# A hybrid decoder block on one core: the left sums of the first MLP product made by accumulating transfers, token loads in lots, m5 over two phases

## The chip, the core and the metric

One Trainium2 chip; the kernel runs on one core of it, as one program. The metric is the device time of one execution in microseconds (us). The core has the matmul engine (PE, with its weight loads PEld), VectorE (DVE), ScalarE (ACT), GpSimd (POOL), and SyncE (SP), which here only issues transfers. A wait in an engine's queue holds everything that stands behind it in that queue.

## What is computed

One decoder layer on x of 2048 tokens by 1024 channels, in float32: two mixers (dilated attention, chunked gMLP), merged by gates and an output product, then a squared-ReLU MLP. Each part has a norm before and behind. The part that the change touches is the MLP:

```
h = _rmsnorm(x, norm_pre_mlp)                         # 2048 x 1024
a = relu(einsum('bsd,df->bsf', h, w_mlp_in))          # 1024 -> 4096
y = einsum('bsf,fd->bsd', a * a, w_mlp_out)           # 4096 -> 1024
x = x + _rmsnorm(y, norm_post_mlp)
```

## The kernel before

**Stages.** Projections and attention; from about 1000 us the gates and the output product, called here the merge (`merge`, `out_block`), over four chunks of 512 tokens in the order 2, 3, 0, 1; from 1406 to 2028 us the first MLP product, the h stage; then the second, the y stage, to the end at 2660.6 us. A float32 product is made of three fp32r matmuls: each operand is split into a high part (a rounded copy, by ACT) and a low part (the difference, by DVE or POOL), and hi*hi, hi*lo and lo*hi are added in PSUM.

**Two levels of Strassen-Winograd.** The h stage replaces eight block products by seven at an outer level, and each of these again by seven. The seven outer products are the *phases*, in the order of `OUTER`: left operands A11, A12, S2, S1, S4, S3, A22, with Winograd numbers m = 1, 2, 6, 5, 3, 7, 4. A11 to A22 are quarters of `w_mlp_in`; S1 to S4 are sums of them. Right operands are quarters of the tokens or sums of them (T). Each phase has eight *steps* (q = 0 to 7, `HQ`), 56 in all (n); a step has seven *products* of six matmuls each (`hproduct`, line 1547). Steps overlap: the list `yorder` gives each product its place, so a step ends six places into the next. A place k is the unit of time of the schedule, and `later(k, f)` puts an instruction at a place.

**Order.** From the end of the merge the order is written out by hand (`as_written`): each engine runs its instructions in program order.

**The left operand of a step.** Before the stage, `w_piece` (13 times in the merge) and `w_load`, `w_sum`, `w_store` (3 times in phase 0) load a pair of weight blocks, make S2, S4, S3 and S1 with four adds, and store them in DRAM (`ws_d`). `load_ha` (line 1380) then brings one left operand of 512 KB into `hraw` (two buffers) with one SP transfer, from `w_mlp_in` or from `ws_d`. `sum_ha` calls `combine`: POOL makes the inner sums (lines 1389, 1390, 1395, 1396, 128x256 each), ACT the high parts (1391, 1397, 1400, 1404), DVE the low parts (1393, 1399, 1402, 1406). It writes `hs`, a ring of three. At the end of step n (place k) the sum of step n+3 is set to places k+1 to k+7 (`SUM_AT`), and the load of step n+5 to k+8. The y stage uses the same `combine` and the same places.

**The right operands of a phase.** `load_hb` (line 1446) brings 2 MB for the next phase in four transfers, all at place 7 of a phase (step 1). Where the operand is a difference (`LESS`, three phases), `less_load` (1450) fetches what is subtracted, 256 KB at a time, and `less_sub` (1454) subtracts it on DVE and POOL, the first 4 or 5 places after. `sum_w2` (POOL, 1474 to 1479) and `ops_hb` (ACT 1467, then DVE or POOL; line 1952 is the `f(*args)` that runs all that `later` holds) make the seven split operands. Most of these are made in the last step of the phase before.

**What becomes of a product.** It is added from PSUM to an accumulator X in SBUF, or in phases m = 2, 5, 3 to a tile `e` (lines 1559, 1561, 1563, mostly DVE). Products of one step share PSUM banks, so a product waits until the last one in its bank, four places before, is read. In phase m = 5 (phase 3, counted from 0), `e` is added to X (DVE and POOL, half each) and stored in `m5_d`; in phases 5 and 6 it is loaded again (`m5_load`, 1579) and subtracted from X (`m5_sub`, POOL, 1584), four tiles a step for eight steps. T sums of tokens come from `t_piece` in the merge and from `outer_load`, `outer_sum`, `outer_store`.

Of the kernel before, what the change touches and what calls it, by code (L numbers as in the profile page):

```python
# [17 lines left out]
P = 128  # L18
# [24 lines left out]
def block_kernel(ctx, tc, a, out):  # L43
# [106 lines left out]
    ws_d = dtile([NF // 4, P, 4, 2, 512], "wsd")  # L150
# [1135 lines left out]
    T_AT, WS_AT = ("T1", "T3", "T4", "T2"), ("S2", "S4", "S3", "S1")  # L1286
# [16 lines left out]
    def w_piece(t):  # L1303

        w, v = (ttp.tile([P, 2, 512], F32, name=f"{n}w{t}", tag=n, bufs=1) for n in ("tq", "tr"))
        for z, n in ((v, t + NF // 2), (w, t)):
            sp.dma_start(z.rearrange("p a c -> p (a c)"), a["w_mlp_in"][n].rearrange("p k c -> p (k c)"))
        yield
        a11, a12, a21, a22 = w[:, 0], w[:, 1], v[:, 0], v[:, 1]
        q, f = divmod(t, 2)  # L1310
        dve.tensor_add(a22, a21, a22)
        dve.tensor_sub(a21, a11, a21)
        pool.dma_start(ws_d[q][:, 2:4, f], v)
        dve.tensor_sub(a11, a22, a11)
        dve.tensor_sub(a12, a12, a11)
        pool.dma_start(ws_d[q][:, 0:2, f], w)
        yield

    W_EARLY = 13
    pieces = deque([w_piece(t) for t in range(W_EARLY - 2)] + [t_piece(0), t_piece(1)] +  # L1320
                   [w_piece(t) for t in range(W_EARLY - 2, W_EARLY)])
# [10 lines left out]

    c_now = [2]

    def merge_pieces(dt):
        if dt in ((0, 2, 4, 6, 7) if c_now[0] == 1 else (1, 3, 5, 7)):
            next_piece()
# [33 lines left out]
    def load_ha(n):  # L1371
        o, q = hsteps[n]
        name = OUTER[o][1]
        raw = hraw_[n] = r4.tile([P, 4, 256], F32, name=f"hraw_{n}", tag="sraw", bufs=2)
# [5 lines left out]
        sp.dma_start(raw.rearrange("p (f k) c -> p f (k c)", f=2), src)  # L1380

    def combine(n, w, raw):
# [11 lines left out]
        yield  # L1394
        pool.tensor_sub(a11, s5, a11)
        pool.tensor_sub(a12, a12, a11)
        act.activation(hi[:, 3], s5, AF.Copy)
        yield
        dve.tensor_sub(lo[:, 3], s5, f32(hi[:, 3]))
        act.activation(hi[:, 4], a21, AF.Copy)  # L1400
        yield
        dve.tensor_sub(lo[:, 4], a21, f32(hi[:, 4]))
        yield
# [36 lines left out]
    def load_hb(o):  # L1440

        name = ("B11", "B21", "T2", "B12", "B22", "B22", "B21")[o]
        for kk in range(2):
            raw = w2r_[o, kk] = l3.tile([P, 5, 512], F32, name=f"hb_{o}{kk}", tag="w2r", bufs=2)
            for kh in range(2):
                sp.dma_start(raw[:, 2 * kh:2 * kh + 2].rearrange("p c t -> p (c t)"), b_rows(name, kk + 2 * kh))
# [16 lines left out]
    def ops_hb(k, o, j, engs):  # L1463
        for m, eng in enumerate(engs):
            hi, lo = w2_[key(o, m), OPS[j]] = spot()
# [46 lines left out]
    def w_load(t):  # L1512

        outer_t["w", t] = [rx.tile([P, 512], F32, name=f"wt{t}{m}", tag="xs" if (t - W_EARLY) % 2 else "c1", bufs=4) for m in range(4)]
        for m, z in enumerate(outer_t["w", t]):
            sp.dma_start(z, a["w_mlp_in"][t + (0, 0, 16, 16)[m]][:, 4 * (m % 2):4 * (m % 2) + 4].rearrange("p k c -> p (k c)"))

    def w_sum(t, which):
        a11, a12, a21, a22 = outer_t["w", t]
        if which == 0:  # L1520
            dve.tensor_add(a22, a21, a22)
        elif which == 1:
            pool.tensor_sub(a21, a11, a21)
        elif which == 2:
            dve.tensor_sub(a11, a22, a11)
        else:
            pool.tensor_sub(a12, a12, a11)

    def w_store(t):
        q, f = divmod(t, 2)  # L1530
        s2, s4, s3, s1 = outer_t.pop(("w", t))
        for m, z in enumerate((s2, s4, s3, s1)):
            sp.dma_start(ws_d[q][:, m, f], z)

    def hproduct(k, n, i):
# [16 lines left out]
        if m in (2, 3, 5):  # L1552
            if first:
                stage_[n, f, c] = rx.tile([P, 512], F32, name=f"e{n}{f}{c}", tag="c1" if (f, c) == (0, 1) else "xs", bufs=4)
            t = stage_[n, f, c]
        else:
            t = x_
        if m in (1, 5) and first:
            act.activation(t, p, AF.Copy)
        elif m in (2, 3) and first:  # L1560
            dve.tensor_add(t, x_, p)
        else:
# [3 lines left out]
        if m == 5:  # L1566
            later(k + 1, (pool if c else dve).tensor_add, x_, x_, t)
# [4 lines left out]
              t.rearrange("p (i c) -> p i c", i=4))  # L1572

# [12 lines left out]
    def hstep(k, n, i):  # L1586
# [3 lines left out]
        if i == 1:  # L1590
            if q == 1:
                if o == 6:
                    for w in range(2):
                        load_w2(w)
                else:
                    load_hb(o + 1)
                    if o + 1 in LESS:
                        for b in range(4):
                            later(k + 6 * b + 1, less_load, o + 1, b)
                            for kk in range(2):  # L1600
                                later(k + 6 * b + 5 + kk, less_sub, o + 1, b, kk)
# [10 lines left out]
        if q == HQ - 1 and USE[i][0] < 6:  # L1612
            j = USE[i][0] + 1
            ops_hb(k, o + 1, j, (dve, dve if o in (0, 3) else pool))
# [4 lines left out]
    def spatial_out(dt):  # L1619
# [12 lines left out]
        merge_pieces(dt)  # L1632
# [16 lines left out]
    for n, c in enumerate(chunks):  # L1649
        if n:  # L1650
            c_now[0] = c
            mg = merge(c, yt, {0: flush, 2: flush}, merge_pieces)
        for i in range(4):
# [3 lines left out]
            if n < 3 or not i:  # L1657
                next_piece()
# [5 lines left out]
            if n == 3 and i == 1:  # L1664
# [25 lines left out]
                for n_ in range(2):  # L1690
                    outer_load(n_)
# [221 lines left out]
    for k in range(7):  # L1913
        at(k, s2)
    for k, f, args in ((0, first_split, (3, 0)), (1, flush, ()), (1, first_split, (3, 1)), (3, first_split, (4, 0)),
                       (4, first_split, (4, 1)), (6, first_split, (5, 0)), (7, first_split, (5, 1)), (7, load_ha, (4,)),
                       (8, first_split, (6, 0)), (9, first_split, (6, 1)), (9, flush, ())):
        later(k, f, *args)
    for n in range(8 + NF // 2 - W_EARLY):
        t = 5 * n - 5  # L1920
        load, one, store, z = (outer_load, outer_sum, outer_store, n) if n < 8 else (w_load, w_sum, w_store, W_EARLY + n - 8)
        if n > 1:
            later(t, load, z)
        for d, m in ((4, 0), (5, 1), (6, 2), (7, 3)):
            later(max(t + d, 0), one, z, m)
        later(t + 9, store, z)
    gfin = None
    for k, (_, stage, n, i) in enumerate(yorder):
# [40 lines left out]
        elif i in (3, ("p", 7)):  # L1969
            m = n + 3 + (NH if stage else 0)  # L1970
            if m < NH + len(ysteps):
# [6 lines left out]
                if m + 2 < NH + len(ysteps):  # L1978
                    later(k + 8, load_raw, m + 2)
# [75 lines left out]
```

## Time and profile before

| what | value |
|---|---|
| runs | 2664.3 us median of 3 (2658.52 to 2667.07) |
| profiled execution | 2662.48 us, its span 2660.6 us, clock granted 0.984 |
| busy | PE 97%, PEld 80%, DVE 69%, POOL 53%, ACT 41% of the span |
| DMA | 568.69 MB, 214 GB/s |
| merge after its first chunk, h stage, y stage | about 1106 to 1406, 1406 to 2028, 2028 to 2640 us |

The trace is of one execution. A row of a view by groups gives the line, engine, operation and tiles, the count behind x, busy us and mean ns of one, and the engine's idle time just before, with what ended it. A row of the timeline gives start and length, and in brackets the idle time before with its releaser. A row of windows gives, for a stretch, each engine's busy us and its instructions, the mean clock granted to PE, the busy share of the DMA engines, and GB/s.

### The profile page before, as it was taken

What the parts mean: (1) busy time and instruction counts of PE and PEld (TensorE: products, weight loads), DVE (VectorE), ACT (ScalarE), POOL (GpSimd) and SP (SyncE); (2) the same over time, 40 slices, a digit from 0 to 9 for tenths busy, and PEclk for the clock granted to TensorE, in tenths of its full rate; (3) what the DMA queues carried; (4) which work ended last, traced back from release to release, by engine and by line L of the source; (5) the groups of instructions that cost most, each with busy time, mean ns of one, the idle gap of its engine ahead of it and who ended that gap; (6) DMA issues with size and microseconds to landing.
All of it is one profiled execution on the core that took longest, in us unless ns stands there. A gap on an engine that the chain in (4) does not pass through costs nothing. (4 is left out here: it accounts for less than half of the span.)

```text
span 2660.6 us, 35654 instructions
## 1 busy us (share of the span) xinstructions
PE 2569.2 (97%) x12122; PEld 2139.0 (80%) x12122; DVE 1835.8 (69%) x3170; ACT 1095.7 (41%) x2318; POOL 1404.9 (53%) x1282
## 2 busy tenths in 40 slices
PE   9999999999999999899999999989889999999998
PEld 8888888888888887788877787867767888888886
DVE  5676665534433465866677888988768888788867
ACT  5213111254455444534435333433224555555555
POOL 0363354374464654111125566857877777777634
PEclk9999999999999999999999999999989999999999
DMA  8779768988888998867677652566764221222236
GB/s 321 283 247 322 266 227 291 301 280 253 291 281 238 242 301 317 317 234 260 232 266 268 197 170 93 178 186 188 235 210 150 88 87 56 88 87 87 88 114 211
DMA packets 412136, 568.69 MB, mean 214 GB/s; under 512 B 58801, under 2 KB 247473, under 8 KB 410930
## 3 DMA queue, kind: packets, MB, share of 16 engines
q1 hardware_dynamic: 385872, 502.63, 58.1%
q0 software_dynamic: 16192, 57.16, 5.5%
q10 hardware_dynamic: 9890, 6.62, 0.8%
q8 instruction: 96, 1.57, 0.2%
q14 instruction: 86, 0.70, 0.1%
HBM read 362.16 MB, written 204.14 MB: 213 GB/s over the span
## 5 line engine op out<-in xcount | busy, mean ns | idle before, releaser
L1547 PE MATMUL ha<-spot,hs 128*128 128x512 f32 x1344 | 345.2, 407 | 43.9 <-DVE X_yt L1563 17.6
L1547 PEld LDWEIGHTS ha<-spot,hs 128*128 128x128 f32 x1344 | 264.2, 198 | 106.4 <-issue 23.7
L1860 PE MATMUL ya<-spot,s 128*128 128x512 f32 x1344 | 325.7, 391 | 3.8 <-DVE X_yt L1868 3.8
L1860 PEld LDWEIGHTS ya<-spot,s 128*128 128x128 f32 x1344 | 253.8, 189 | 57.0 <-ACT sraw L1724 4.2
L1547 PE MATMUL hc<-spot,hs 128*128 128x512 f32 x672 | 175.0, 396 | 8.3 <-DVE X_xr L1563 3.4
L728 PE MATMUL g<-opA,spots 128*128 128x512 f32 x672 | 171.5, 399 | 1.8 <-DVE cv L760 1.8
L1860 PE MATMUL yc<-spot,s 128*128 128x512 f32 x672 | 170.6, 389 | 0.0
L1724 ACT ACTIVATE sraw<-sraw 128x1024 f32<-128x1024 f32 x128 | 134.4, 1050 | 83.5 <-DMA sraw<-sd 78.1
L728 PE MATMUL g<-opB,spots 128*128 128x512 f32 x648 | 164.0, 397 | 0.0
L1547 PEld LDWEIGHTS hc<-spot,hs 128*128 128x128 f32 x672 | 129.0, 193 | 37.9 <-DVE X_xr L1563 3.9
L96 PE MATMUL x<-hT_a,wq 128*128 128x512 f32 x384 | 149.7, 390 | 0.0
L97 PE MATMUL x<-hT_a,wq 128*128 128x512 f32 x384 | 149.4, 389 | 0.0
L98 PE MATMUL x<-hT_a,wq 128*128 128x512 f32 x384 | 149.4, 389 | 0.0
L1860 PEld LDWEIGHTS yc<-spot,s 128*128 128x128 f32 x672 | 126.4, 188 | 26.3
L728 PEld LDWEIGHTS g<-opA,spots 128*128 128x128 f32 x672 | 121.6, 189 | 24.1 <-issue 2.2
L79 POOL TENSOR_TENSOR spots<-gr,spots 128x512 fp32r<-128x512 f32 x98 | 127.8, 1308 | 22.1 <-PE g L728 7.9
L79 POOL TENSOR_TENSOR spot<-w2r,spot 128x512 fp32r<-128x512 f32 x79 | 120.9, 1553 | 34.7 <-ACT spot L71 34.7
L728 PEld LDWEIGHTS g<-opB,spots 128*128 128x128 f32 x648 | 116.9, 188 | 21.2
L71 ACT ACTIVATE hl<-r 128x512 fp32r<-128x512 f32 x48 | 30.4, 633 | 237.0 <-POOL r L329 89.0
L978 DVE TENSOR_REDUCE o<-po 128x256 f32<-128x512 f32 x48 | 33.2, 691 | 133.9 <-PE po L977 133.9
L73 POOL TENSOR_SCALAR spots<-gr 128x512 fp32r<-128x512 f32 x86 | 55.4, 644 | 132.0 <-PE g L728 93.4
L73 POOL TENSOR_SCALAR wq<-wq_r 128x1024 fp32r<-128x1024 f32 x24 | 31.9, 1335 | 138.2 <-PE va L98 87.6
(463 smaller groups left out, 6863.6 us busy)
## 6 DMA issues: line engine op xcount, KB each, us to landing
sraw<-sd SPq DMA_DIRECT2D x128, 256.0 KB, 3.3
qk<-hl SPq DMA_DIRECT2D x24, 1024.0 KB, 5.6
qq<-qk SPq DMA_DIRECT2D x96, 256.0 KB, 5.1
sd<-e SPq DMA_DIRECT2D x64, 256.0 KB, 4.7
hraw<-wsd SPq DMA_DIRECT2D x32, 512.0 KB, 4.5
w2r<-in_w_mlp_out_dram SPq DMA_DIRECT2D x16, 1024.0 KB, 6.5
g<-gated SPq DMA_DIRECT2D x56, 256.0 KB, 5.6
gr<-sgd SPq DMA_DIRECT2D x53, 256.0 KB, 4.8
```

Source lines behind the costliest of these rows:

```text
L71: act.activation(hi, src, AF.Copy)
L73: pool.tensor_scalar(hi, src, 1.0, 1.0, op0=OP.mult, op1=OP.mult)
L79: (pool if lo_eng == "pool" else dve).tensor_sub(lo, src, f32(hi))
L96: pe.matmul(ps, lh, rh, start=start, stop=False)
L97: pe.matmul(ps, lh, rl, start=False, stop=False)
L98: pe.matmul(ps, ll, rh, start=False, stop=stop)
L728: pe.matmul(p, w[:, l, k], h[:, r, k], start=i in (1, 6, 5, 4) and not k and not m, stop=k == 3 and m == 2, skip_group_check=True)
L978: dve.tensor_reduce(ot[:, :, j * 64:(j + 1) * 64], po.rearrange("p (b h e) -> p b e h", b=4, h=2), axis=AX.X, op=OP.add)
L1547: pe.matmul(p, w[:, l, S_AT[i], kk * P:(kk + 1) * P], b[r], start=i in (1, 2, 5) and not kk and not z, stop=kk == 1 and z == 2, skip_group ...
L1724: act.activation(sraw_[n], sraw_[n], func)
L1860: pe.matmul(p, s[:, l], w[r], start=i in (1, 2, 5) and not m and not o, stop=m == 1 and o == 2, skip_group_check=True)
```

## The change

1. `w_piece`, `w_load`, `w_sum`, `w_store` and `ws_d` go. In the merge only the two `t_piece` stay, in the four blocks of the third chunk. The eight `outer_load` groups start at place 4 and come every 5 places (before: two ahead of the stage, the rest from place 5).
2. `load_ha` takes terms. The first comes over SP; the others are added onto the tile by transfers that POOL issues with `accum_op=OP.add`. S2 = A21 + A22 - A11, S1 = A21 + A22, S4 = A12 - S2, S3 = A21 - A11. S3 has the other sign than before, so the products of m = 7 are subtracted. The load moves from k+8 to k+6; the added terms are at k+9 and k+12.
3. The negatives of A11 and S2 are made by `negate` on ACT at the start of `sum_ha` in phase A11 and phase S2 (one 128x1024 into an X tile that is not in use yet, or two 128x512), and stored over SP (512 KB a step, 16 steps).
4. `combine` takes five places instead of seven.
5. `load_hb` is cut into four: places 4, 8, 11 and 15 of a phase. `less_load` starts at place 16 and comes every 5 places instead of 6; each `less_sub` is 4 places behind its load.
6. Of the second split operand, one half is made in step 6 instead of step 7, on POOL instead of DVE in most phases.
7. In phase m = 5 the half that POOL added to X is added by an accumulating transfer inside SBUF (`collect`), issued by POOL. `e` tiles are spread evenly over two tags.
8. `m5_load` and `m5_sub` come every 9.5 places instead of 7: from step 44 to the end of step 54.

```diff
-    ws_d = dtile([NF // 4, P, 4, 2, 512], "wsd")
+    neg_d = {name: dtile([NF // 4, P, 2, 512], f"neg{name}d") for name in ("A11", "S2")}
...
-    pieces = deque([w_piece(t) for t in range(W_EARLY - 2)] + [t_piece(0), t_piece(1)] +
-                   [w_piece(t) for t in range(W_EARLY - 2, W_EARLY)])
+    pieces = deque([t_piece(0), t_piece(1)])
...
+    TERMS = dict(S2=("A21", "A22", "-A11"), S1=("A21", "A22"), S4=("A12", "-S2"), S3=("A21", "-A11"))
+
+    def load_ha(n, term=0):
         o, q = hsteps[n]
+        terms = TERMS.get(OUTER[o][1], (OUTER[o][1],))
+        if term >= len(terms):
+            return
+        name = terms[term]
...
-            src = ws_d[q][:, WS_AT.index(name)]
-        sp.dma_start(raw.rearrange("p (f k) c -> p (f k) c", f=2), src)
+            src = neg_d[name[1:]][q]
+        if term:
+            pool.dma_start(raw, src, accum_op=OP.add)
+        else:
+            sp.dma_start(raw, src)
+
+    def negate(n):
+
+        o, q = hsteps[n]
+        name, raw = OUTER[o][1], hraw_[n]
+        dst = neg_d[name][q].rearrange("p f c -> p (f c)")
+        if name == "A11" and q > 1:
+            z = [X[(0, 0, 8, 9, 12, 13, 14, 15)[q]]]
+        else:
+            z = [rx.tile([P, 512], F32, name=f"neg{n}{m}", tag="xs", bufs=4) for m in range(2)]
+        w = D // len(z)
+        for m, t in enumerate(z):
+            act.activation(t, raw.rearrange("p k c -> p (k c)")[:, m * w:(m + 1) * w], AF.Copy, scale=-1.0)
+        return [(dst[:, m * w:(m + 1) * w], t) for m, t in enumerate(z)]
...
-        yield from combine(n, w, hraw_.pop(n))
-
-    SUM_AT = (1, 2, 3, 4, 5, 6, 7)
+        kept = negate(n) if OUTER[hsteps[n][0]][1] in neg_d else []
+        yield from staged(combine(n, w, hraw_.pop(n)), kept)
...
+    SUM_AT = (1, 2, 3, 4, 5)
...
-            later(k + 1, (pool if c else dve).tensor_add, x_, x_, t)
+            if c:
+                later(k + 1, collect, x_, t)
+            else:
+                later(k + 1, dve.tensor_add, x_, x_, t)
...
+    def collect(to, t):
+        pool.dma_start(to, t, accum_op=OP.add)
...
-            q5 = n - 5 * HQ - 3
-            if 0 <= q5 < HQ:
-                for f in range(2):
-                    later(k + 3 * f, m5_load, q5, f)
-                    later(k + 4 + 2 * f, m5_sub, q5, f)
...
+        if i == 6 and not q and o < 6:
+            for m in range(4):
+                later(k + (0, 4, 7, 11)[m], load_hb, o + 1, *divmod(m, 2))
+            if o + 1 in LESS:
+                for m, b in enumerate((0, 1, 3, 2)):
+                    later(k + 12 + 5 * m, less_load, o + 1, b)
+                    for kk in range(2):
+                        later(k + 16 + 5 * m, less_sub, o + 1, b, kk)
+        if i == 6 and q == 6:
+            ops_hb(k, o + 1, 1, (dve if o in (0, 3) else pool, None))
...
+    for q in range(HQ):
+        t = 7 * (5 * HQ + 4) + 19 * q // 2
+        for f in range(2):
+            later(t + 5 * f, m5_load, q, f)
+            later(t + 5 * f + 5, m5_sub, q, f)
...
-                    later(k + 8, load_raw, m + 2)
+                    later(k + 6, load_raw, m + 2)
+                    if m + 2 < NH:
+                        later(k + 9, load_ha, m + 2, 1)
+                        later(k + 12, load_ha, m + 2, 2)
```

More of the change, by code (lines that the diff above doesn't have):

```diff
@@ L1438, in b_rows, with load_hb @@
         return h2_d[:, k + (4 if name[1] == "2" else 0), t0 + c.start * 512:t0 + c.stop * 512]
-    def load_hb(o):
+    def load_hb(o, kk, kh):
         name = ("B11", "B21", "T2", "B12", "B22", "B22", "B21")[o]
[L1443 to L1446, printed above, removed]
+        if not kh:
+            w2r_[o, kk] = l3.tile([P, 5, 512], F32, name=f"hb_{o}{kk}", tag="w2r", bufs=2)
+        sp.dma_start(w2r_[o, kk][:, 2 * kh:2 * kh + 2].rearrange("p c t -> p (c t)"), b_rows(name, kk + 2 * kh))
     def less_load(o, b):
@@ L1464, in ops_hb @@
         for m, eng in enumerate(engs):
+            if not eng:
+                continue
             hi, lo = w2_[key(o, m), OPS[j]] = spot()
@@ L1510, in b_out @@
         return tq_d[:, n % 4, n // 4 * 512:(n // 4 + 1) * 512]
[L1512 to L1533, printed above, removed]
     def hproduct(k, n, i):
@@ L1656, in block_kernel @@
             last.append(b)
-            if n < 3 or not i:
+            if n == 2:
                 next_piece()
```

86 lines of the change are left out of this document (29 added, 57 removed).

## The prediction

> **What bounds the kernel now.** I read the page first, then the stretches, who PE waits for, and the timelines around the longest waits.
>
> ```profile
> span 2660.6 us, 35654 instructions
> PE 2569.2 (97%) x12122; PEld 2139.0 (80%) x12122; DVE 1835.8 (69%) x3170; ACT 1095.7 (41%) x2318; POOL 1404.9 (53%) x1282
> ```
>
> PE is the bound, so the change can pay only where PE stands or runs slowly. The stretches are the merge after its first chunk, the seven phases of the h stage, and the y stage:
>
> ```profile
> core 0: us, PE busy (x) PEld busy (x) DVE busy (x) ACT busy (x) POOL busy (x), PEclk, DMA share, GB/s
> 1106.00:1406.00 300.00, 290.79 (x1317) 239.00 (x1316) 206.63 (x417) 132.06 (x265) 57.03 (x81) 0.99 0.72 250
> 1406.00:1500.00 94.00, 82.46 (x355) 66.84 (x353) 78.32 (x108) 48.26 (x94) 57.20 (x53) 0.96 0.72 246
> 1500.00:1579.00 79.00, 78.95 (x336) 65.13 (x337) 66.29 (x98) 25.36 (x47) 44.94 (x44) 0.96 0.60 181
> 1579.00:1663.00 84.00, 78.43 (x337) 64.44 (x336) 69.95 (x99) 25.42 (x47) 57.44 (x52) 0.96 0.36 116
> 1663.00:1749.00 86.00, 77.48 (x338) 62.84 (x337) 80.44 (x83) 41.03 (x77) 74.02 (x60) 1.00 0.49 160
> 1749.00:1835.00 86.00, 81.07 (x338) 66.45 (x339) 73.46 (x104) 25.57 (x46) 53.97 (x50) 0.94 0.64 193
> 1835.00:1930.00 95.00, 81.41 (x336) 65.75 (x334) 71.03 (x99) 24.54 (x45) 77.92 (x66) 0.93 0.75 231
> 1930.00:2028.00 98.00, 88.38 (x355) 70.25 (x356) 73.25 (x104) 31.77 (x55) 78.78 (x69) 0.93 0.65 201
> 2028.00:2640.00 612.00, 608.24 (x2673) 503.15 (x2672) 481.31 (x695) 329.05 (x562) 406.13 (x373) 0.99 0.29 99
> ```
>
> The y stage sets the scale: 612 us for 2673 matmuls, 0.229 us each. A phase of 8 x 7 x 6 = 336 matmuls at that pace is 76.9 us, a place of the schedule (six matmuls) 1.37 us, a step 9.6 us. The seven phases take 622 us instead of 538: 84 us are lost, 17 in phase 0, 2, 7, 9, 9, then 18 and 21 in phases 5 and 6. (Phases 0 and 6 hold some 19 matmuls of their neighbours, 4 us each, so 76 are to be had.) The merge has 9 us of idle PE, the y stage 4. Who ends PE's waits there:
>
> ```profile
> PE ha L1547 <- DVE X_yt L1563: 17.6, 6, 5.6
> PE ha L1547 <- DVE e L1561: 13.8, 3, 6.2
> PE b L96 <- DVE g L1208: 5.5, 3, 3.0
> PE ha L1547 <- DVE X_gpost L1563: 5.3, 1, 5.3
> PE hc L1547 <- DVE X_xr L1563: 3.4, 1, 3.4
> ```
>
> It is DVE, late with emptying PSUM, in few long waits. But DVE is 71 to 94% busy there, so the question is what held its queue:
>
> ```profile
> 1603.90 1.62 PE L1547 MATMUL ha<-spot,hs 128*128 128x512 f32 x3 [5.57 <-DVE X_yt L1563]
> 1775.97 2.05 PE L1547 MATMUL ha<-spot,hs 128*128 128x512 f32 x4 [4.55 <-DVE e L1561]
> 1859.43 1.62 PE L1547 MATMUL ha<-spot,hs 128*128 128x512 f32 x3 [5.56 <-DVE X_yt L1563]
> ...
> DVE hb L1454 <- DMA hb<-tqd: 8.6, 2, 8.1
> DVE hb L1454 <- DMA hb<-h2d: 8.0, 1, 8.0
> DVE hb L1454 <- DMA m5d<-e: 5.9, 1, 5.9
> ...
> 1604.00:1608.00 4.00, 4.00 (x10) 3.14 (x11) 4.00 (x7) 1.23 (x3) 2.01 (x3) 0.50 0.77 262
> ```
>
> Three of the waits are one event in phases 2, 4 and 5: the first token subtraction stands in DVE's queue 5.9 to 8.1 us for its transfer, behind the 2 MB that were just asked for, and the PSUM reads stand behind it. After the gap PE runs 4 us at a granted clock of 0.50, ten matmuls where 17.5 fit: 1.7 us more per gap. A DVE block of 8 us costs PE 5.6, of 5.9 us 4.55: the first 1.4 to 2.5 us are free.
>
> ```profile
> 1909.67 0.60 DVE L1399 TENSOR_TENSOR hs<-fifth,hs 128x256 fp32r<-128x256 f32 x1 [8.78 <-ACT hs L1397]
> L1584 POOL TENSOR_TENSOR X_yt<-X_yt,m 128x512 f32<-128x512 f32 x12 | 18.8, 1597 | 0.8 <-DMA m<-m5d 0.8
> ```
>
> In phases 5 and 6 it is POOL: 77.9 and 78.8 us busy where 76.9 is the pace. Its m5 subtractions at 1.6 us push `combine`'s first sums back; ACT waits for these, DVE 8.78 us for ACT, PE for DVE.
>
> **Merge (term -5).** Off go 13 pieces with four DVE adds each:
>
> ```profile
> L1314 DVE TENSOR_TENSOR tqw<-trw,tqw 128x512 f32<-128x512 f32 x13 | 8.9, 687 | 0.1
> 1347.11 0.69 DVE L1295 TENSOR_TENSOR tq<-tq 128x512 f32<-128x512 f32 x1 [4.46 <-DMA tq<-h2d]
> 1348.46 0.50 PE L96 MATMUL b<-yt,wb 128*128 128x512 f32 x1 [3.03 <-DVE g L1208]
> ```
>
> That is 52 x 0.687 = 36 us of DVE, all but the 9 us beside a busy PE. One wait surely goes: DVE stood 4.46 us for `t_piece`'s load, PE 3.03; now a whole output block lies between that load and its sums. With half of the other g waits (5.5 - 3.0) and some slow clock: -5, bounds 0 and -9.
>
> **Token loads in lots (term -18).** Three gaps, 5.57 + 4.55 + 5.56 = 15.7, and 3 x 1.7 of slow clock: -20.8 if nothing is late behind them. The first subtraction is now five places (6.9 us) behind the last lot's issue and four (5.5 us) behind its own load. I leave 1 us each: -18, bounds -9 and -20.8.
>
> **Phase 0 (term -5).**
>
> ```profile
> L1525 DVE TENSOR_TENSOR wt<-wt,wt 128x512 f32<-128x512 f32 x3 | 3.1, 1035 | 1.2 <-POOL wt L1523 1.2
> L1523 POOL TENSOR_TENSOR wt<-wt,wt 128x512 f32<-128x512 f32 x3 | 5.1, 1700 | 6.9 <-DVE wt L1521 6.9
> ```
>
> The three late pieces, two such DVE adds (6.2 us) and two POOL adds (10.2 us), leave the end of the phase, where DVE is full and PE waits 3.4 us (X_xr). The negatives come on ACT, which is busy 48 of 94 us, and their 16 stores on SP, off any path that PE waits for; if ACT were late they would cost their own 1.2 us a step. -5, bounds 0 and -9.
>
> **Phase 3 (term -4).**
>
> ```profile
> L1952 POOL TENSOR_TENSOR X_yt<-X_yt,e 128x512 f32<-128x512 f32 x6 | 9.4, 1573 | 4.0 <-DVE e L1563 4.0
> L1313 POOL DMA_DIRECT2D wsd<-trw x13 | 9.3, 713 | 97.5 <-DVE trw L1312 97.5
> ```
>
> POOL gives up 16 x 1.57 = 25 us of adds for 16 issues at 0.71 (11 us), and one split leaves DVE's last step. DVE's SBUF adds ran beside POOL's there. The phase loses 9 us, 6.2 of it in the wait at its end (e, longest): -4, bounds 0 and -8.
>
> **Phases 5 and 6 (term -9).** m5 moves 8 of its 32 subtractions, 8 x 1.6 = 12.8 us, from phase 5 to 6. POOL then has 77.9 - 12.8 + 3 (one split, a few added terms) = 68 in phase 5 and 78.8 + 12.8 + 2 = 93.6 in phase 6. Phase 5, 95 us less the 7.3 counted with the lots, can come down to some 82: -6. Phase 6 is then held near 94 by POOL alone instead of 98: -3. Bounds +5 (POOL's lag of 17 us passes to PE whole) and -20 (POOL's ops shorten as DVE thins out, and the lag ends in the y stage).
>
> **The accumulating left operands (term +8).** Nothing like them is in the trace. S2 is a chain: load, add, add, and `combine` must then release the tile (two of them), so it must turn over in two steps, 19.2 us.
>
> ```profile
> 1908.47 0.72 POOL L1389 TENSOR_TENSOR fifth<-hraw 128x256 f32<-128x256 f32 x1
> 1912.49 1.10 DVE L1406 TENSOR_TENSOR hs<-hraw,hs 128x512 fp32r<-128x512 f32 x1
> ...
> hraw<-in_w_mlp_in_dram SPq DMA_DIRECT2D x24, 512.0 KB, 4.0
> wsd<-trw POOLq DMA_DIRECT2D x13, 512.0 KB, 4.7
> ...
> L1559 ACT ACTIVATE e<-ha 128x512 f32<-128x512 f32 x32 | 18.8, 594 | 24.5 <-PE ha L1547 17.8 <-issue 5.0 <-POOL X_xr L1952 1.4
> SPq L1446 <- POOL spot L1952: 20.8, 3, 7.7
> ```
>
> A pressed `combine` takes 5.1 us from its first sum to its last read (1908.47 to 1913.59), the negatives 2 x 0.6, the load 4.0. An added term needs at least the 4.7 of a POOL transfer of its size; since it also reads the tile, up to double, 9.4. I take 5.5, near the row that exists. Turnover 5.1 + 1.2 + 4.0 + 2 x 5.5 = 21.3, 2.1 too long in two steps, 1.05 x 8 steps = 8. At 4.7 it is 2; at 9.4, 40 (29.1 - 19.2 = 9.9 in two steps). The 24 steps with one added term need 5.1 + 4.0 + 5.5 = 14.6, which fits, even with 9.4 (18.5).
>
> The Trainium skill's page DMA: Bandwidth & Descriptors (Anatomy of one DMA) gives a transfer about 2.0 us plus its bytes at 436 GB/s; by that, as an estimate, 512 KB take 3.2 us, S2 fits in its two steps, and this term would be nothing and the total 8 us better. The rows for this size, 4.0 and 4.7, are longer, so I keep them.
>
> **POOL and SP in order (terms +3 and +2).** An added term stands in POOL's queue until the term before it has landed; it is three places (4.1 us) behind the load's place, and the load takes 4.0 once SP gets to it. Behind it stand that step's two `hraw` sums, then ACT and DVE. 40 waits, mostly short: +3, bounds 0 and +20 (half a microsecond each). The first lot stands in SP's queue before the last split of its tile is made, so SP waits there, with an `hraw` load behind it; SP waited up to 7.7 us at line 1446 already. +2, bounds 0 and +6. The y stage has no idle to give; `combine` in five places costs 0 while DVE and ACT keep their lead there, up to +5 if not.
>
> **Sum.** -5 - 18 - 5 - 4 - 9 + 8 + 3 + 2 = -28. On the profiled execution's 2662.48 us (span 2660.6 and 1.9 around it) that is 2634.5; the median of the runs stands 1.8 us above it, so I say 2635.
>
> **Rivals.**
> - *Better*: terms land in 4.7, POOL's lag runs out in the y stage. -9 - 20.8 - 9 - 8 - 15 + 2 = -60: 2603. For it speaks that long waits feed on each other here (gap, slow clock); against, POOL's 93 us in phase 6.
> - *Slower*: an added term lands in about 10.5 us, because it reads the tile as well and shares the queues. S2 turns over in 5.1 + 1.2 + 4.0 + 21 = 31.3, +48 over 8 steps; the other 24 need 19.6, +5. In place of the +8 that gives +17 against the old kernel: 2680. It decides from about 9 us a term (4 x (10.3 + 2 x 9 - 19.2) = 36, what the rest gives).
> - *Given back*: POOL, blocked in order by landings and by issues (40 + 16 at 0.71 = 40 us that its phases 1 to 4 did not have), becomes what DVE waits for in every step from S2 to S3, by about one issue, 0.75 us: +24 over those 32 steps, 2659. For it: POOL is the weak engine there already; against: 45 to 57 us of 77 in phases 1, 2 and 4.
> - *The lots do not do what they say*: SP, held at the first lot, sends them in one burst again. The -18 go: 2653.
>
> **Numbers.** Chances: the sum 0.50, better 0.18, slower 0.12, given back 0.15, burst 0.05. A measurement of this kernel can tell about 0.3%, 8 us. Faster by more: 0.50 + 0.18 + 0.05 and a little of "given back", 0.75. Same: most of "given back", 0.12. Slower: 0.13. The range leaves out the slower rival and little else: 2602 to 2668.
>
> **What would show it.** Right: no DVE wait on `hb` above 2 us at line 1454's successor and no 5 us PE gap in phases 2, 4, 5; wsd gone; phase 5 near 82 us, phase 6 near 94 with POOL over 85 busy; S2's operands 1 us late a step. Wrong: accumulating transfers landing in 9 us or more, ACT's first high part waiting for `hraw` in steps 14 to 21, POOL idle before its hraw sums because of a landing, phases 1 and 2 over 90 us, or new waits in the y stage.

## The result and the profile after

The changed kernel takes 2692.59 us (median of 4 runs, 2690.21 to 2695.86), the kernel before, beside it, 2665.69 (2658.52 to 2673.3). The ratio is 1.0101, 95% interval [1.0071, 1.0132]: slower by 1.0%. Forecast were 2635 us and a gain; 2692.6 lies above the range too.

The head of the page, then the stretches (the merge, the seven phases by their first and last matmul, the y stage):

```profile
span 2691.3 us, 35656 instructions
...
PE 2580.0 (96%) x12122; PEld 2140.5 (80%) x12122; DVE 1788.6 (66%) x3107; ACT 1110.7 (41%) x2342; POOL 1381.2 (51%) x1295
```

```profile
core 0: us, PE busy (x) PEld busy (x) DVE busy (x) ACT busy (x) POOL busy (x), PEclk, DMA share, GB/s
1106.00:1390.70 284.70, 284.70 (x1314) 236.85 (x1313) 178.89 (x372) 133.76 (x269) 39.02 (x56) 1.00 0.51 174
1390.70:1473.10 82.40, 79.05 (x354) 64.30 (x352) 66.58 (x95) 51.87 (x98) 46.55 (x45) 1.00 0.75 263
1473.10:1561.60 88.50, 80.29 (x337) 65.50 (x337) 70.64 (x96) 22.30 (x42) 46.13 (x47) 0.94 0.67 183
1561.60:1681.30 119.70, 92.16 (x336) 71.73 (x337) 70.22 (x99) 35.02 (x66) 68.40 (x66) 0.86 0.71 172
1681.30:1778.70 97.40, 82.47 (x337) 65.27 (x335) 68.92 (x84) 40.54 (x77) 70.00 (x70) 0.95 0.89 223
1778.70:1868.30 89.60, 81.39 (x336) 64.76 (x336) 70.42 (x101) 25.66 (x46) 56.98 (x57) 0.96 0.93 239
1868.30:1966.40 98.10, 84.06 (x337) 66.45 (x337) 69.97 (x99) 24.40 (x45) 70.04 (x65) 0.93 0.82 230
1966.40:2064.80 98.40, 86.08 (x353) 67.70 (x354) 77.53 (x102) 31.41 (x54) 93.11 (x79) 0.97 0.71 220
2064.80:2670.00 605.20, 605.20 (x2671) 500.95 (x2670) 478.78 (x694) 333.39 (x563) 393.69 (x373) 1.00 0.29 100
```

The h stage begins 15.7 us earlier (1390.7 for 1406.4), and PE has no idle time in the merge. Phase 0 falls from 93.6 to 82.4. All of that and more is lost in the phases that follow: phases 1 to 5 took 79, 84, 86, 85 and 95 us and take 88.5, 119.7, 97.4, 89.6 and 98.1. In phase 2, where S2 is used, PE runs at a granted clock of 0.86, its busy time rises by 14 us for the same matmuls, and it stands 27.5 us besides. The y stage is faster: 0.2266 us a matmul for 0.2290, and 626 us from the last matmul of the h stage to the end where it was 633. One wait of PE is gone there; the kernel before had

```profile
PE ya L1860 <- DVE X_yt L1868: 3.8, 1, 3.8
```

Who ends PE's waits:

```profile
PE hc L1534 <- DVE X_yt L1552: 13.5, 3, 9.5
PE hc L1534 <- DVE e L1552: 10.8, 4, 6.2
PE ha L1534 <- ACT e L1546: 10.8, 4, 4.5
```

DVE, as before, but for another reason. No DVE wait for an `hb` transfer is left, so the 5.9 to 8.1 us blocks of before are gone. In their place POOL stands, waiting for left operands to land (us, times, longest; the h stage), 92.6 us in 26 waits:

```profile
POOL fifth L1393 <- DMA hraw<-negA11d: 42.3, 11, 6.7
...
POOL hraw L1364 <- DMA hraw<-in_w_mlp_in_dram: 40.6, 12, 5.3
...
POOL fifth L1393 <- DMA hraw<-negS2d: 9.7, 3, 6.0
```

Two S2 steps in its timeline (start, length, in brackets the idle time before and its releaser):

```profile
1596.65 0.72 POOL L1393 TENSOR_TENSOR fifth<-hraw 128x256 f32<-128x256 f32 x1 [6.56 <-DMA hraw<-negA11d]
...
1598.61 1.23 POOL L1364 DMA_DIRECT2D hraw<-in_w_mlp_in_dram  x1
...
1604.87 0.91 POOL L1364 DMA_DIRECT2D hraw<-negA11d  x1 [3.22 <-DMA hraw<-in_w_mlp_in_dram]
...
1611.40 0.74 POOL L1393 TENSOR_TENSOR fifth<-hraw 128x256 f32<-128x256 f32 x1 [4.30 <-DMA hraw<-negA11d]
...
1627.36 0.72 POOL L1393 TENSOR_TENSOR fifth<-hraw 128x256 f32<-128x256 f32 x1 [6.73 <-DMA hraw<-negA11d]
```

From one step's first sum (`fifth`) to the next one's are 14.75 and 15.96 us, where 9.6 is the pace. Between them POOL waits twice for a landing: the second added term waits for the first, the next `fifth` for the second. The transfers, then the issues on POOL (ns, min/median/max):

```profile
hraw<-in_w_mlp_in_dram SPq DMA_DIRECT2D x56, 512.0 KB, 5.0
...
hraw<-in_w_mlp_in_dram POOLq DMA_DIRECT2D x16, 512.0 KB, 5.9
hraw<-negA11d POOLq DMA_DIRECT2D x16, 512.0 KB, 7.1
...
hraw<-negS2d POOLq DMA_DIRECT2D x8, 512.0 KB, 5.9
```

```profile
L1364 POOL DMA_DIRECT2D hraw<-in_w_mlp_in_dram x16: 1196/1218/1248, 1532.8 to 1741.3; - x16
L1364 POOL DMA_DIRECT2D hraw<-negA11d x16: 866/898/926, 1539.0 to 1930.8; - x16
L1364 POOL DMA_DIRECT2D hraw<-negS2d x8: 873/874/897, 1755.2 to 1838.6; - x8
```

An added term lands in 5.9 to 7.1 us (medians; 5.5 was taken). The rule of the Trainium skill's page DMA: Bandwidth & Descriptors (Anatomy of one DMA) gives, as an estimate, 3.2 us for a transfer of 512 KB; the rows of these accumulating ones, about twice that, do not bear it out here.

### The profile page after: what moved, and what is told of

Its sections match the earlier page's. It is cut to its first block, busy times and chain, and to the rows that moved or that the text cites. A ratio compares the mean times of both kernels' runs of the same rounds, so it can differ in the third digit from the quotient of the medians.

```text
span 2691.3 us, 35656 instructions
## 1 busy us (share of the span) xinstructions
PE 2580.0 (96%) x12122; PEld 2140.5 (80%) x12122; DVE 1788.6 (66%) x3107; ACT 1110.7 (41%) x2342; POOL 1381.2 (51%) x1295
## 5 line engine op out<-in xcount | busy, mean ns | idle before, releaser
L1534 PE MATMUL ha<-spot,hs 128*128 128x512 f32 x1344 | 351.8, 411 | 43.9 <-ACT e L1546 10.8
L1534 PE MATMUL hc<-spot,hs 128*128 128x512 f32 x672 | 183.1, 410 | 40.7 <-DVE X_yt L1552 13.5
L79 POOL TENSOR_TENSOR spots<-gr,spots 128x512 fp32r<-128x512 f32 x98 | 128.7, 1317 | 20.8 <-DMA gr<-in_w_in_dram 7.0
L79 POOL TENSOR_TENSOR spot<-w2r,spot 128x512 fp32r<-128x512 f32 x79 | 112.3, 1444 | 45.3 <-ACT spot L71 45.3
L1397 DVE TENSOR_TENSOR hs<-hraw,hs 128x768 fp32r<-128x768 f32 x56 | 64.0, 1143 | 76.4 <-ACT hs L1395 76.4
```

The lines of the kernel that those rows point to most:

```text
L79: (pool if lo_eng == "pool" else dve).tensor_sub(lo, src, f32(hi))
L1397: dve.tensor_sub(lo[:, :3], raw[:, :3], f32(hi[:, :3]))
L1534: pe.matmul(p, w[:, l, S_AT[i], kk * P:(kk + 1) * P], b[r], start=i in (1, 2, 5) and not kk and not z, stop=kk == 1 and z == 2, skip_group ...
```

## Experiments

Each run is compared with runs of the kernel before on the same chip. The first theory was: POOL's queue, in order, puts both landings of S2 between two first sums.

**S2 without its third term.**

```diff
-    TERMS = dict(S2=("A21", "A22", "-A11"), S1=("A21", "A22"), S4=("A12", "-S2"), S3=("A21", "-A11"))
+    TERMS = dict(S2=("A21", "A22"), S1=("A21", "A22"), S4=("A12", "-S2"), S3=("A21", "-A11"))
```

> The third term of S2 (-A11) is left out, so S2 and what follows from it are not the reference's sums; all else stays, the negatives and their stores too. Theory 'one step': in POOL's queue the two added terms of one operand and the first sum of the operand before it stand in one row per step, 1.9 + 5.9 + 7.1 = 15 us where a step is 9.6. With one added term the row is 7.8 us and fits: phases 1 and 2 come from 88 + 120 to about 80 + 86, the kernel to about 2650. Theory 'two tiles' (the tile's turnover, sum 6 + load 5 + two terms 13 = 24 us in two steps of 9.6 each, is too long): 17 us, fits as well, about 2650. Theory 'negatives' (ACT's negations and their stores, and the DMA traffic, hold the phase): phase 2 stays over 110, about 2685.

2662.74 us, 1.0001 [0.999, 1.0012]: 30 us less than the changed kernel, though not the 2650 of the first two theories. Phase 2 falls to 90.5, so 'negatives' (over 110) is out; phases 3 to 5 gain nothing. Eight of the 40 issues and their bytes went with the term.

**A third `hraw` buffer** (in place of one pair of split buffers, item 6 undone).

```diff
+            hraw_[n] = l3.tile([P, 4, 256], F32, name=f"hraw_{n}", tag="hraw", bufs=1) if n % 3 == 2 else \
+                r4.tile([P, 4, 256], F32, name=f"hraw_{n}", tag="sraw", bufs=2)
```

> hraw gets three tiles instead of two (paid with one split tile, so that the second operand's halves are made in the last step again, as before the change). All added terms stay at their places. 'Two tiles': the turnover of 24 us now has three steps, 28.8 us; phase 2 falls from 120 to about 90, the kernel to about 2660. 'One step': POOL's order is the same, first sum, added term, added term, first sum, so phase 2 stays within 5 us of 120 and the kernel within 8 us of 2692.

2695.36, 1.0123 [1.0105, 1.0142]. Its S2 steps in POOL's timeline:

```profile
1602.61 0.72 POOL L1394 TENSOR_TENSOR fifth<-hraw 128x256 f32<-128x256 f32 x1 [4.87 <-DMA hraw<-negA11d]
...
1612.72 0.91 POOL L1365 DMA_DIRECT2D hraw<-negA11d  x1 [5.12 <-DMA hraw<-in_w_mlp_in_dram]
...
1618.32 0.73 POOL L1394 TENSOR_TENSOR fifth<-hraw 128x256 f32<-128x256 f32 x1 [3.37 <-DMA hraw<-negA11d]
```

15.7 us a step, two landings in it, with three buffers as with two. With the issues at these places the buffers were not the limit: the order of POOL's queue was.

**No added terms** (S2, S1 and S3 read as A21, S4 as A12).

```diff
+    TERMS = dict(S2=("A21",), S1=("A21",), S4=("A12",), S3=("A21",))
```

> No term is added at all: S2, S1 and S3 are read as A21 and S4 as A12, so these four left operands are not the reference's; negatives, their stores and everything else stay. This is what the rest of the change is worth. All theories in which the added terms are the loss: h stage near 570 us instead of 674, kernel at 2600 to 2625. If the loss is elsewhere (order of combine, lots, m5): above 2660.

2606.98, 0.9791 [0.9776, 0.9806]. The rest of the change is worth some 56 us, and the 40 added terms take 86, not the 11 of the forecast: against this run the changed kernel loses 8, 42, 13, 11 and 12 us in phases 1 to 5.

**S3 made in phase 0 and stored**, so that S2 = A22 + S3 has one added term and S3 none; a POOL transfer adds A21 onto each tile of negatives in phase 0.

```diff
+    TERMS = dict(S2=("A22", "+S3"), S1=("A21", "A22"), S4=("A12", "-S2"), S3=("+S3",))
```

> Computes the reference's sums in another way: in phase 0 POOL adds A21 onto the negative of A11 (in the X tile, off the hraw tiles) and S3 = A21 - A11 is stored in place of -A11; S2 = A22 + S3 then needs one added term and S3 none. 'One step' and 'two tiles': phase 2 near 88, phase 5 a few us better, phase 0 and 1 no more than 4 us worse: kernel at 2640 to 2655, faster than before the change. 'Negatives': above 2680.

2660.73, 0.9994 [0.9982, 1.0006]. Phase 2 is 88.2, but phase 0 grew from 82.4 to 101.1: eight of the terms had only moved there, a miss.

**Three buffers, each operand begun a step earlier.** The third buffer as above, and:

```diff
+                    later(k + 6, load_ha, m + 3)
+                    later(k + 10, load_ha, m + 3, 1)
+                    later(k + 16, load_ha, m + 3, 2)
```

> three_raw, and with its third tile every left operand is begun a step earlier: load of step n+6 at k+6, added terms at k+10 (behind the hraw sums of the step before, not ahead of them) and k+16, first sum at k+22. Theory 'POOL's order': no landing (5.9 to 7.1 us) stands between two first sums any more; phase 2 falls from 119 to under 90, phases 3 and 4 by 5 to 10 each, the kernel from 2695 to 2625 to 2645. If the transfers themselves (their bytes beside the loads, or POOL's 0.9 to 1.2 us for each) are what costs, phase 2 stays over 105 and the kernel over 2675.

2664.12, 1.0011 [0.9999, 1.0023]. Against the run with the third buffer alone phase 2 fell from 119 to 102, and phases 3 and 5 from 95 each to 87 and 89, yet the 2625 to 2645 of the theory was missed by 20 us. Either the chain was not all of it, or it was not gone: POOL still stood 21.4 us at its issues until transfers from `w_mlp_in` had landed.

**The terms one place later, alone and with S3 stored.**

```diff
-                        later(k + 9, load_ha, m + 2, 1)
-                        later(k + 12, load_ha, m + 2, 2)
+                        later(k + 10, load_ha, m + 2, 1)
+                        later(k + 13, load_ha, m + 2, 2)
```

> The changed kernel, its added terms one place later (k+10 and k+13), so that in POOL's queue the two inner sums a11 and a12 of step n+4 stand ahead of the first added term of step n+5, which waits for its load to land. Theory 'in order': in the phases with one added term (3, 4, 5) those two sums no longer wait for a landing, the step comes down from some 10.4 us to 9.6, and phases 3 to 5 (97, 90, 98 us) give back 5 or so each; S2 keeps its two landings per step; total about 2678 (2665 to 2686). Rival 'too late': the term now lands after the place of its step's first sum; 2695 to 2705. Rival 'traffic and issues', order does not matter: 2693 within 4.

> The kernel with S3 made and stored in phase 0 (so that S2, S1 and S4 have one added term each and S3 none), with its added terms one place later, at k+10. Theory 'in order': as in the run with the terms one place later, phases 2 to 4 lose most of their wait for a landing ahead of a11 and a12: 2660.7 less 10 to 20, about 2645. Rival 'too late' or 'traffic and issues': 2660 within 4, or up to 2670.

2722.81, 1.0229 [1.0207, 1.0251], and 2675.25, 1.0046 [1.003, 1.0063]: 30 and 15 us worse than at k+9. Later is worse, as 'too late' said, but both lie above every forecast (2705 and 2670 at most), and nothing foresaw 145 us in phase 2. What the first one's trace holds besides is taken up below, under where an issue stands.

**The same 40 transfers off the chain.** They add onto a DRAM array that nobody reads.

```diff
+                pool.dma_start(neg_d["A11"][(q + 4 * (term - 1)) % HQ],
+                               a["w_mlp_in"][f0:f0 + 2, :, 0:4].rearrange("f p k c -> p f (k c)"), accum_op=OP.add)
```

> The kernel without added terms (single quarters stand for the sums S1 to S4, so the product is another one), to which the 40 accumulating transfers are added again at their old places, of the same 512 KB and issued by POOL, but onto a DRAM array that nobody reads: issue time, traffic and POOL's share of work are there, and no left operand waits for a landing. Theory 'chain': the cost of the added terms is the waiting for landings in POOL's queue, so this stays near the kernel without them, 2607 plus at most 20: 2607 to 2627. Rival 'traffic and issues': 40 issues of about 1 us and 21 MB read and added are themselves the cost: 2660 to 2690.

2663.75, 1.0009 [0.9995, 1.0023]. That is in the range of 'traffic and issues': the 40 transfers cost 57 us with no left operand waiting for an added term, so landings are not all of the 86. By phases the changed kernel loses against this run 25.6 us in phase 2, 3.6 in phase 3, and within 2 elsewhere: 29 in all, nearly all in S2. But 29 and 57 are no clean shares of the 86, as this run pays for something else (waits in the h stage):

```profile
POOL hb L1466 <- DMA hb<-h2d: 29.8, 4, 10.3
POOL hb L1466 <- DMA hb<-tqd: 18.5, 2, 12.7
```

The changed kernel waits 11.5 us there, and DVE not at all, which here stands 23.8 us for the same transfers. In phases 4 and 5 the two kernels take the same time by different waits: the changed one has POOL stand 20 and 18 us for left operands, this one 3 and 1. What the landings and what issue and traffic cost the operands with one term in the changed kernel is not shown; the earlier start above, which gave phases 3 and 5 some 7 us each, speaks for the landings too.

**Issue without bytes, bytes without POOL's issue.**

```diff
+                pool.dma_start(neg_d["A11"][(q + 4 * (term - 1)) % HQ][:, :, :8],
+                               a["w_mlp_in"][f0:f0 + 2, :, 0, 0:8].rearrange("f p c -> p f c"), accum_op=OP.add)
...
+                sp.dma_start(neg_d["A11"][(q + 4 * (term - 1)) % HQ],
+                             a["w_mlp_in"][f0:f0 + 2, :, 0:4].rearrange("f p k c -> p f (k c)"))
```

> As the run with the 40 transfers off the chain (2663.8 us; single quarters stand for S1 to S4), but each of the 40 accumulating transfers carries 8 KB instead of 512 KB, in the same 256 pieces. Theory 'issue': the 42 us that the 40 issues take of POOL are the cost; it stays at 2650 to 2664, if an issue still takes about 1 us. Theory 'traffic': the bytes on the DMA queues, which make token loads and left operands land later, are the cost: 2607 to 2620. In between, the two share it by the number.

> As the run with the 40 transfers off the chain, but SP issues them, as plain copies of the same 512 KB (no addition, so the target is not read): traffic without POOL's issue. Theory 'issue': 2607 to 2622. Theory 'traffic': 2640 to 2664.

2634.52, 0.9899 [0.9884, 0.9914], and 2619.71, 0.9841 [0.9826, 0.9855]. Against the 2607 without terms: 27.5 us for the issues, 12.7 for plain bytes, 57 for issues and added bytes together. The 17 us beyond the sum of the two are either what adding to the target, here in DRAM, puts on top of the traffic, or what the two do to each other; no run tells these apart. In the run off the chain, the group of issues, and two rows of transfers with that of the run without terms behind them:

```profile
L1355 POOL DMA_DIRECT2D negA11d<-in_w_mlp_in_dram x40 | 42.2, 1055 | 0.0
```

```profile
negA11d<-in_w_mlp_in_dram POOLq DMA_DIRECT2D x40, 512.0 KB, 8.0
hb<-h2d SPq DMA_DIRECT2D x20, 512.0 KB, 7.9
```

```profile
hb<-h2d SPq DMA_DIRECT2D x20, 512.0 KB, 6.6
```

An issue takes as long for 8 KB (42.2 us for 40 there too, in as many pieces) as for 512. With the bytes the token loads land 1.3 us later; in the changed kernel they take 6.7. With the issues of 8 KB, ACT's waits for POOL's last inner sums grow from 116.9 to 145.1 us, 53 waits in both: that is where POOL's 42 us seem to go.

**Where an issue stands.** With 8 KB, DVE and POOL at the end of phase 1:

```profile
1536.68 5.36 DVE L1412 TENSOR_TENSOR hs<-hraw,hs 128x512 fp32r<-128x512 f32 x1 [0.70 <-ACT hs L1410]
```

```profile
1535.93 1.06 POOL L1355 DMA_DIRECT2D negA11d<-in_w_mlp_in_dram  x1
1536.57 1.75 POOL L1491 TENSOR_TENSOR hb<-hb 128x512 f32<-128x512 f32 x1
1537.82 1.74 POOL L1945 TENSOR_TENSOR spot<-hb,spot 128x512 fp32r<-128x512 f32 x1
1539.06 1.74 POOL L1491 TENSOR_TENSOR hb<-hb 128x512 f32<-128x512 f32 x1
1540.30 1.18 POOL L1397 TENSOR_TENSOR fifth<-hraw 128x256 f32<-128x256 f32 x1
```

A DVE subtraction of 1.1 us takes 5.36, and ends 0.6 us behind POOL's run of sums. Behind the issue POOL's rows overlap by 0.5 us, just ahead of it they do not (spans on POOL are rough). Two more such cases lie in this run, 15 in the run begun a step earlier, each begun within 0.8 us of an issue. The Trainium skill's page SBUF — State Buffer (Who interferes with whom) says that a DVE instruction with two SBUF inputs contends with a GpSimd instruction that reads SBUF; the long DVE rows beside the terms' issues all have two SBUF inputs. By that rule a DVE instruction waits for the POOL instruction that holds the pair; here the long row covers a run of four. Two runs move such issues ahead of the two dependent sums a11 and a12, the one with 8 KB and the one begun a step earlier:

```diff
-                        later(k + 12, load_ha, m + 2, 2)
+                        later(k + 9, load_ha, m + 2, 2)
...
-                    later(k + 10, load_ha, m + 3, 1)
+                    later(k + (9 if OUTER[hsteps[m + 3][0]][1] == "S2" else 16), load_ha, m + 3, 1)
```

> As the run with 8 KB transfers off the chain (2634.5 us; single quarters stand for S1 to S4), but the second transfer of each S2 step is issued at k+9 instead of k+12, so that both stand ahead of the two dependent sums a11 and a12. In that run three DVE instructions took 5.36, 5.55 and 4.58 us instead of 1.1 to 1.8, each begun within 0.8 us of a POOL issue that is followed by POOL adds which do not depend on each other. Theory 'DVE held': such a run of POOL adds right behind an issue keeps DVE's two-operand adds waiting until POOL itself waits; with the issues ahead of dependent sums these three are gone and phases 1 and 2 get back some 12 us: 2620 to 2626. Rival 'issue time': 40 issues of 1 us cost what they cost wherever they stand: 2632 to 2637.

> The run with a third buffer and the operands begun a step earlier (2664.1 us), its added terms moved: the only term of S1, S4 and S3 to k+16 and the first of S2 to k+9 (both were at k+10), the second of S2 stays at k+16, so that each issue stands ahead of the dependent sums a11 and a12 and none ahead of a run of independent POOL adds. In that run 16 DVE instructions took over 2.5 us, 77 us together, 14 of them begun beside such an issue. Theory 'DVE held': most of these are gone, some 50 us of DVE, of which PE gets back about half: 2635 to 2645, below the kernel before. Rival 'landings': the landings and the traffic set the time, no change, 2660 to 2668; or S2's first term at k+9 holds POOL for its load again, 2670 to 2690.

2628.07, 0.9869 [0.9855, 0.9884], and 2655.93, 0.9971 [0.9959, 0.9983]: 6 and 8 us better, more than the rivals' nothing and less than the 8 to 14 and 19 to 29 expected. The low part's subtraction in the run with 8 KB and with the issue moved (ns, min/median/max), then the 128x256 one in the run begun earlier and with its issues moved:

```profile
L1412 DVE TENSOR_TENSOR hs<-hraw,hs x54: 675/1100/5361, 1404.2 to 1979.9; 128x512 fp32r<-128x512 f32 x54
```

```profile
L1412 DVE TENSOR_TENSOR hs<-hraw,hs x54: 676/1103/3273, 1405.0 to 1974.1; 128x512 fp32r<-128x512 f32 x54
```

```profile
L1406 DVE TENSOR_TENSOR hs<-hraw,hs x51: 409/682/8130, 1407.6 to 1985.0; 128x256 fp32r<-128x256 f32 x51
```

```profile
L1406 DVE TENSOR_TENSOR hs<-hraw,hs x53: 411/956/1741, 1403.1 to 1985.7; 128x256 fp32r<-128x256 f32 x53
```

The long rows go: DVE instructions over 2.5 us in the h stage fall from 5 to 2 and from 15 to 2 (the changed kernel has 2); those that are left stand behind issues of `collect`. Phase 1 gives back 6.4 and 7.4 us, phase 2 of the second run 9, while its phases 3 and 5, whose terms now land later, lose 5 and 3. So DVE is held where an issue stands ahead of such a run of sums, and with 8 KB the move brings 6 of the 27 us of issue; how much of the 6 is DVE alone was not measured. The kernel with the terms one place later has 15 such rows too, so its 30 us need not be lateness alone; how much is which was not measured.

**The other parts, put into the kernel before one by one:** lots alone, m5 over two phases alone, no weight pieces (plain loads in place of the sums), lots and m5 together.

> The kernel before with the token loads in lots alone (with the new places of less_load and less_sub). The prediction's term: -18, so 2645. If the waits only move to another place: within 8 us of 2663.

> The kernel before with m5 spread over two phases alone. The prediction's term: phase 5 down by 6, phase 6 by 3, the kernel at 2654. If POOL's lag only moves to phase 6: phase 5 down by 10 or more, phase 6 up by as much, the kernel within 5 us of 2663.

> The kernel before without the weight pieces: S2, S1, S3 are read as A21 and S4 as A12, so these left operands are not the reference's; t_piece sits where the change has it. What leaving the pieces out is worth: the prediction had -5 in the merge and -5 in phase 0, 2653; the profile after the change shows the h stage beginning 15.7 us earlier and phase 0 11 us shorter, which would make 2637.

> The kernel before with the token loads in lots and m5 over two phases, and its weight pieces kept. If the two gains (0.9963 and 0.9966 alone) add up: ratio 0.993, some 2647. If the same wait is counted in both (both touch phase 5): 0.995 or above, 2652.

0.9963 [0.9949, 0.9977], 0.9966 [0.9952, 0.998], 0.9893 [0.9878, 0.9907] and 0.9926 [0.9902, 0.995]: some 10, 9, 28 and 20 us, where 18, 9, 10 (26 by the trace of the changed kernel) and 16 were expected. Lots and m5 add up. Phases 2, 4 and 5 with lots alone, then phases 5 and 6 with m5 alone:

```profile
1579.00:1655.20 76.20, 76.20 (x338) 63.10 (x337) 70.28 (x99) 25.90 (x47) 58.85 (x52) 1.00 0.40 128
...
1742.60:1827.60 85.00, 80.32 (x336) 65.73 (x337) 73.89 (x103) 25.48 (x46) 54.63 (x49) 0.95 0.64 193
1827.60:1921.60 94.00, 82.53 (x338) 65.20 (x336) 73.75 (x99) 24.51 (x45) 79.34 (x66) 0.95 0.73 234
```

```profile
1833.20:1920.80 87.60, 79.56 (x337) 64.69 (x335) 69.26 (x99) 23.77 (x44) 64.18 (x56) 0.96 0.75 227
1920.80:2022.70 101.90, 86.66 (x354) 67.65 (x355) 76.28 (x103) 32.18 (x56) 92.82 (x79) 0.97 0.69 214
```

With lots alone phase 2 gains 8.0 us, phases 4 and 5 0.3 and 1.5. In phase 4 the wait has moved: DVE stands 5.1 us ahead of an `e` tile whose last store to `m5_d`, issued 0.4 us behind the first lot, has not landed, and PE 4.65 behind it:

```profile
DVE e L1560 <- DMA m5d<-e: 5.1, 1, 5.1
```

With m5 alone phase 5 falls by 7.9 us and phase 6 grows by 4.5.

**All of the change but its first part:** weight pieces and plain loads of S1 to S4 stay. Then the same with two of the four adds of a merge piece on POOL:

```diff
-        dve.tensor_sub(a21, a11, a21)
+        pool.tensor_sub(a21, a11, a21)
...
-        dve.tensor_sub(a12, a12, a11)
+        pool.tensor_sub(a12, a12, a11)
```

> The change without its first part: the weight pieces, their DRAM array and plain loads of S1 to S4 are kept; lots, m5 over two phases, the accumulating transfers inside SBUF, the split made in step 6, combine in five places and the load at k+6 are all there. If the parts add up: the kernel without added terms, 2607, plus the later start of the h stage (1403.9 against 1390.6) and the longer phase 0 (91 against 82): 2629 (2622 to 2640). Rival: combine in five places and the earlier load only help where nothing else loads: 2642, as with lots and m5 alone.

> The run with the sums kept, and two of the four adds of each of the 13 weight pieces of the merge on POOL instead of DVE. POOL was busy 57 of 300 us in the merge; DVE loses 26 x 0.69 = 18 us. If DVE's queue is what the pieces cost PE there: 5 to 10 us better, about 2622. Rival: POOL's longer adds (1.6 us) hold its stores and what waits for them, or DVE is slowed beside POOL: no change or worse, 2629 to 2635.

2637.65, 0.9908 [0.9893, 0.9923]: faster than both kernels. Its phases 3 to 5 (phases 1 and 2 take 78.1 and 77.5):

```profile
1657.10:1740.70 83.60, 77.62 (x338) 62.63 (x336) 69.35 (x83) 41.07 (x78) 61.94 (x61) 1.00 0.73 210
1740.70:1819.00 78.30, 78.19 (x337) 64.25 (x338) 70.89 (x102) 25.94 (x46) 53.28 (x49) 0.98 0.74 220
1819.00:1904.60 85.60, 79.01 (x337) 63.69 (x335) 68.12 (x98) 24.27 (x45) 66.61 (x59) 0.98 0.74 226
```

As in the kernel without terms (80, 78, 84, 78, 86 in phases 1 to 5). The 8 us above the expected 2629 are a start at 1408.5 and 103.7 us in phase 6. Two adds on POOL in its merge made it 2647.44, 0.9949 [0.9932, 0.9966]: worse, as the rival said and by more; DVE's adds are the cheaper ones here.

## Why the prediction was wrong

- **The step that failed** is the pair "the accumulating left operands (term +8)" and "POOL in order (+3, bounds 0 and +20)": 11 us forecast, 86 measured. The working said that the tile "must turn over in two steps, 19.2 us", and added up the stations of one buffer. But POOL takes part in every step, and in its queue the first term of the next operand stands behind this step's `fifth`, which waits for its own second term: both landings fall into one step. With the 2.0 us from the first sum to the first issue (1596.65 to 1598.61) and the forecast's 2 x 5.5 of landing a step is 13.0 instead of 9.6, some 27 us in eight; with the landings measured, 5.9 and 7.1, it is 15.0, and eight are 120, where phase 2 took 119.7. The kernel without the third term and the one with a third buffer show it.
- **The operands with one term** "need 5.1 + 4.0 + 5.5 = 14.6, which fits": that again counted the buffer and not the queue. "40 waits, mostly short", half a microsecond each at most, became 92.6 us in which POOL stands for left operands, all terms together.
- **Issue and traffic** had no price in the sum. The issue on POOL (1.0 us on average, where a plain one of that size took 0.71) was set against POOL's 45 to 57 us of 77 in phases 1, 2 and 4, as if the rest were free. Off the chain issue and traffic alone cost 57 us. How the 44 us that the added terms cost in phases 1, 3, 4 and 5 divide between landings, issue and traffic stays open.
- **The rivals.** "Slower" asked for landings of 9 us or more; they are 5.9 to 7.1, so its threshold, built on two steps a turn, was wrong while its sign was right. "Given back" named the issues and priced them at 24 us; the run with 8 KB measured 27.5. Of the signs of being wrong, "POOL idle before its hraw sums because of a landing" is what the trace shows.
- **Merge and phase 0** (-5 and -5, bounds -9 each): the h stage starts 15.7 us earlier and phase 0 is 11.2 shorter; without weight pieces alone, -28. The bound counted PE's idle time, 9 us in the merge; its busy time fell as well, 290.79 for 1317 matmuls to 284.70 for 1314.
- **Lots** (-18, bound -9): some 10 came with lots alone, 8 of them in phase 2. DVE's long blocks at the token subtraction go as said in phases 2 and 4 and shrink to 3.3 us in phase 5, but in phase 4 5.1 us of waiting come back at a store of `m5_d`, a step the working did not have, and phase 5 gives 1.5. With the whole change but its first part DVE waits 3.4 us for `m5_d`, and phase 4 is 78. The `e` tiles spread over two tags may do that; it wasn't tried.
- **Phases 5 and 6** (-9): with m5 alone the kernel gains 9, but that is luck in part: phase 5 gives 7.9 and phase 6 takes 4.5 of it back, where 6 and 3 more were forecast; the rest of the 9 lies outside these phases. POOL's 93.6 us in phase 6 came out at 93.1, but PE's phase 6 took 98.4, not 94.
- **Phase 3** (-4): 83.6 for 86.1 where the sums are kept. **The y stage** (0, "no idle to give"): 6.5 us shorter. It had the 4 us of idle PE that the working itself names. All runs with `combine` in five places and the earlier load take 626 us from the h stage to the end, with the sums kept too; all without take 631 to 633. Which of them does it was not tried.

Without the added terms the forecast's terms make -39, the run -56: 27 come ahead of phase 1, 22 net in phases 1 to 6, 6.5 in the y stage. The one part with no row of its own in the trace of before decided the sign.

## What to carry to other kernels

A chain of accumulating transfers that a compute engine issues in its own order can cost its landings once per step of that engine; a third buffer alone did not help here, and with each operand begun a step earlier it gave 31 us back. Trace the queue, not the buffer. Each such transfer also took 0.9 to 1.2 us of the issuing engine, and its bytes cost something beside that. The 40 were dearer here (86 us) than the weight pieces with their 64 adds that they replaced (some 28). An engine that is idle a third of a phase is no cover if others wait for it where the new work falls: put that work into its timeline.

## What the runs showed of the hardware

- An accumulating transfer of 512 KB landed in 5.9 to 7.1 us into SBUF (medians of the changed kernel) and 8.0 from DRAM into DRAM (the run off the chain), beside 5.0 for a plain load over SP. Its issue took POOL 1.05 us off the chain, for 512 KB and for 8 KB in as many pieces.
- With such an issue just ahead of independent POOL sums, a DVE instruction with two SBUF inputs took 2.7 to 8.1 us in 15 cases of the run begun a step earlier, where its like takes 0.4 to 1.8. With the issue ahead of dependent POOL sums this was gone. What holds DVE there was not measured.
- In phase 2 of the changed kernel the granted clock was 0.86 on the mean over 120 us, and PE was busy 92.2 us for matmuls that take 76.6 at a clock of 1.00 in the run without added terms.
